# GLA's key and query projections among the convolved tiles, and both halves of an HGRN head's level tree together

## The chip, the cores and the metric

The kernel runs on one core of a Trainium2 chip. The metric is the time of one execution in microseconds of the device, the median of several runs. The profiles are of single executions of the same program, with the records of every engine: TensorE (PE, its weight loads PEld), VectorE (DVE), ScalarE (ACT), GpSimd (POOL) and the engine that issues the DMAs (SP).

## The reference

A two-layer encoder trunk over 1024 tokens of width 1024, float32. Each layer projects the residual stream into the inputs of four token mixers, which run on the same input; each mixer's output is gated, the four are concatenated (2048 wide), projected back and normalized.

```
for i in range(DEPTH):
    h = einsum('bsd,dn->bsn', x, w_in[i])            # all mixers' inputs
    y_a = attention_branch(...)                      # 8 heads of 64, 2 key heads, softmax over 1024
    y_h = hgrn2_branch(...)                          # 4 heads, 128 wide, gated scan in both directions
    y_s = ssd_branch(...)                            # Mamba-2: depthwise convolution, then a scan both ways
    y_g = gla_branch(...)                            # 4 heads, keys of 64, gated scan both ways
    out = einsum('bsn,nd->bsd', concatenate(...), w_out[i])
    x = layer_norm(ALPHA * x + out, ln_g[i], ln_b[i])
```

The gated scan of HGRN and GLA is `S_t = diag(exp(g_t)) S_{t-1} + k_t v_t^T`, `o_t = S_t^T q_t`, forward and backward, summed.

## The kernel before

All time runs along the free dimension: a tile of 128 channels by 512 tokens is one half, and everything is done for half 0 (tokens 0 to 511) and half 1. A projection of 128 channels (`proj` with a PSUM tile of both halves, `projh` with one tile a half) multiplies each 128x128 block of weights with the stream as a high and a low part: `whi` by `xh`, `whi` by `xl`, `wlo` by `xh`, 8 blocks each, 24 matmuls of 512 columns a half. A weight tile comes by DMA (`wraw`), ACT makes `whi`, POOL makes `wlo`. Most results are stored to DRAM (`hdr`) and loaded again by the mixer that needs them.

**The stages of a layer**: attention; HGRN, head after head; SSD; GLA; and the output projection (`oproj`), in pieces by half and branch, which runs beside GLA. Then the LayerNorm and the next layer.

**The level tree** (`tree`, line 649) is how HGRN and GLA do the scan inside chunks of 128 tokens. For one half of a head it makes 32x32 products of keys and queries on TensorE (`lv`), first for single positions (`lv<-q,ks`), then for level sizes 1, 2, 4, 8, 16; for 32 and 64 the products are 64 wide. After each level VectorE multiplies keys (`M`, `C`), queries (`QP`) and decays (`T`) on to the next level and copies a masked part of the products into `near`, while ACT copies a part of `C` into the new `M`. The next level's products read the new `M` and `QP`. `scan_unit` (line 722) does it for half 1 (`second_half`, then its backward states), then for half 0 (`rest`), then the states and the output `ot`. `nh` is the number of heads in the 128 channels: 1 for HGRN, 2 for GLA.

**What sets the order.** The engines' queues are in order, and the program that writes the instructions is a planner. Projections are items of one list, `fill`; the mixers' steps are generators in twelve lanes. A generator yields a list of what its next instructions need: tiles, free PSUM banks ("A:2" is two free banks of the small kind), free buffers ("k2:4"), conditions. The planner keeps a clock for each engine out of fixed costs by size (class `Plan`, line 130) and estimates from it when each tile is ready (`when`, line 547). `run` (line 591) takes a mixer's step when that time has come by TensorE's planned clock, and a step of the current projection otherwise. A yield is no wait on the chip; it only decides what is emitted first. The real waits come from the data.

**The other places that the change touches.** `s_conv` (line 1257) projects one of eight tiles of SSD's input and convolves it: one ACT pass and four VectorE passes over 1024 columns. `s_mix` (line 1377) does the scan of two SSD heads: states `sP` out of `xw` (POOL), the part inside chunks `yd`, the part of the states `yo`; VectorE multiplies `yo` by `off` into `ytmp`, and POOL adds `ytmp` to the sum `u`. `h_stat` (line 1075) normalizes HGRN's output on VectorE and multiplies it by the gate on POOL. `spill` (line 1101) projects a tile with one PSUM tile of both halves, `spill_halves` (line 1112) with one for each half; both store it.

The list of GLA's early projections is line 32:

```
AFILL = ("gk", "gq")
```

Those four tiles stand in `fill` behind GLA's gate tiles and may run as soon as the layer's stream is there (line 1898); the planner used two of them in HGRN of layer 0, and in layer 1 one ahead of HGRN and two in it.

Of the kernel before, what the change touches and what calls it, by code (L numbers as in the profile page):

```python
# [31 lines left out]
AFILL = ("gk", "gq")  # L32
# [285 lines left out]
def hybrid_trunk(ctx, tc, xT_d, wt_d, wo_d, pk_d, w2_d, gain_d, masks_d, imask_d, tri_d, ident_d, rope_d, lnr_d, out_d):  # L318
# [330 lines left out]
    def tree(ins, nh, out):  # L649
        T1, Mk, C, q = ins  # L650
        ins.clear()
        kk = 128 // nh
# [4 lines left out]
        yield [ks, q, f"A:{nh}"]  # L657
# [17 lines left out]
        yield [Mk, QP, f"A:{nh}"]  # L675
# [3 lines left out]
        for lvl, h in enumerate(LEVELS):  # L679
# [39 lines left out]
            yield [M2, QP] + ([f"A:{nh}"] if h < 32 else [])  # L719
        out.update(QP=QP, M=Mk, C=C, T=T, AT=AT)  # L720

    def scan_unit(halves, nh, emit_o):
# [32 lines left out]
        def second_half():  # L755
            yield halves[1][0]
            yield from tree(halves[1][0], nh, un[1])
            yield from states(1, 1, None, Sb)
            first[0] = True

        def rest():
            yield halves[0][0]
            yield from tree(halves[0][0], nh, un[0])
# [63 lines left out]
    def layer(li):  # L827
# [10 lines left out]
        def pc(name, j=0):  # L838
            o = PK[name][0] + j
            return pk[:, o:o + 1]  # L840
# [234 lines left out]
        def h_stat():  # L1075
            for hf in (0, 1):
                r = yield from rstd_of(("o", hf), "hss", 1.0 / (128 * 512), math.log(0.5 * 128.0 ** -0.5))
                for n in range(4):
                    yield ["k2:5"]
                    z = load(("hz", n), hf, "zs")  # L1080
                    o = load(("o", n), hf, "o")
                    yield [z, o, r]
                    ve.scalar_tensor_tensor(out=o, in0=o, scalar=pc("hnorm", n), in1=r, op0=ALU.mult, op1=ALU.mult)
                    tt(gp, o, o, z, ALU.mult)
                    store_y(512 + n * 128, hf, o)
# [291 lines left out]
        def s_mix(n):  # L1377
            def gen():
# [43 lines left out]
                for hf in (0, 1):  # L1422
# [12 lines left out]
                    for d, Ss in ((0, Sf), (1, Sb)):  # L1435
# [7 lines left out]
                        tb = k2("ytmp")  # L1443
                        tt(ve, tb[:, z], yo[:, z], offb[d][:, z], ALU.mult)
                        tt(gp, ta[:, z], ta[:, z], tb[:, z], ALU.add)
# [444 lines left out]
        for g in range(2):  # L1890
            F(f"sB{li}{g}", s_conv(4 + g), after=[f"hp{li}3"], ws=[wsrc("sB", g)])
            F(f"sC{li}{g}", s_conv(6 + g), after=[f"hp{li}3"], ws=[wsrc("sC", g)])
            for n in (2 * g, 2 * g + 1):
                F(f"sx{li}{n}", s_conv(n), after=[f"hp{li}3"], ws=[wsrc("sx", n)])
        for nm in ("gz",):
# [13 lines left out]
        for nm, kind, cnt in (("gk", "raw", 2), ("gq", "raw", 2), ("gv", "tok", 4), ("sz", "silu", 4)):  # L1909
# [101 lines left out]
```

## Time and profile before

| what | value |
|---|---|
| median of 3 runs | 2555.42 us (2553.99 to 2556.37) |
| the profiled execution's own time | 2557.98 us |
| its span, first to last instruction | 2556.2 us |
| TensorE busy | 2420.9 us, 95% |
| VectorE, ScalarE, POOL busy | 1642.6, 1074.9, 971.6 us |
| mean granted TensorE clock | 0.981 |
| HBM read, written | 205.39 MB, 75.96 MB |

A row of a group has the engine, the operation, what it writes and reads, the shape and the count; then the busy time of the group in us, the mean of one in ns, the idle time of the engine just before, and who ended it. A row of the time line has the start and the length in us of one instruction or of a run of equal ones, and in brackets the idle time before it. Matmuls overlap in these records: what one costs is the distance from its start to the next one's. A row of busy time by stretch has, for each engine, busy us and instructions, then the granted clock, the DMA engines' share and GB/s. A matmul in float32 counts as two instructions, so 16 products of a level are `x32`.

### The profile page before, as it was taken

How to read it: one execution, taken by the hardware profiler on the slowest of the kernel's cores; microseconds unless marked ns; L12 is line 12 of the kernel's file. 1: busy time of each engine (PE TensorE's matmuls, PEld its weight loads, DVE VectorE, ACT ScalarE, POOL GpSimd, SP SyncE). 2: the span in 40 equal slices, each digit the busy share in tenths (PEclk: the TensorE clock that was granted, in tenths of full speed). 3: DMA queues.
4: the chain of work that ended last, by engine and by line, in shares of the span. 5: the costliest groups of instructions: out<-in, count | busy, mean ns of one | idle time of the engine just before them, and what ended most of it. 6: DMA issues, size and time to landing. Idle time of an engine off the chain costs nothing. (4 is left out here: it accounts for less than half of the span.)

```text
span 2556.2 us, 46533 instructions
## 1 busy us (share of the span) xinstructions
PE 2420.9 (95%) x18352; PEld 1828.7 (72%) x18352; DVE 1642.6 (64%) x2975; ACT 1074.9 (42%) x2092; POOL 971.6 (38%) x820
## 2 busy tenths in 40 slices
PE   8999999999999996999899999999999999998995
PEld 6767556777778885667777675557777788876774
DVE  2467755453488779774644686554645787887756
ACT  4564555333334334244345545443333243443442
POOL 4432111222225456454464331122223236574444
PEclk9999999999999998999999999999999999999998
DMA  6222111111126547643252311111111156687332
GB/s 222 96 92 66 54 54 46 38 51 51 42 92 213 183 140 277 203 128 97 92 184 80 108 49 59 58 46 38 50 42 51 63 180 203 197 270 235 109 100 91
DMA packets 170174, 284.39 MB, mean 111 GB/s; under 512 B 17780, under 2 KB 43380, under 8 KB 169956
## 3 DMA queue, kind: packets, MB, share of 16 engines
q1 hardware_dynamic: 169956, 281.41, 33.7%
q8 instruction: 145, 2.38, 0.4%
q14 instruction: 73, 0.60, 0.1%
HBM read 205.39 MB, written 75.96 MB: 110 GB/s over the span
## 5 line engine op out<-in xcount | busy, mean ns | idle before, releaser
L312 POOL TENSOR_TENSOR wlo<-wraw,whi 128x512 fp32r<-128x512 f32 x372 | 523.9, 1431 | 716.9 <-ACT whi L312 677.0
L312 PE MATMUL proj<-xh,whi 128*128 128x512 f32 x1056 | 430.4, 408 | 5.1 <-ACT whi L312 5.1
L312 PE MATMUL proj<-xl,whi 128*128 128x512 f32 x1056 | 414.1, 392 | 0.0
L312 PE MATMUL projh<-xh,whi 128*128 128x512 f32 x704 | 289.4, 411 | 16.0 <-ACT whi L312 14.7
L312 PE MATMUL projh<-xl,whi 128*128 128x512 f32 x704 | 281.1, 399 | 1.0 <-DVE xl L312 1.0
L312 PE MATMUL proj<-xh,wlo 128*128 128x512 f32 x1056 | 280.9, 398 | 0.0
L312 ACT CAST whi<-wraw 128x512 fp32r<-128x512 f32 x372 | 213.7, 622 | 114.7 <-DMA wraw<-in_wt 53.6
L312 PEld LDWEIGHTS proj<-xh,whi 128*128 128x128 f32 x1056 | 199.0, 188 | 53.7 <-issue 7.0
L312 PEld LDWEIGHTS proj<-xl,whi 128*128 128x128 f32 x1056 | 199.2, 189 | 38.0 <-issue 1.0
L312 PE MATMUL oproj<-mxh,whi 128*128 128x512 f32 x512 | 216.3, 422 | 9.5 <-ACT whi L312 8.8
L312 PEld LDWEIGHTS proj<-xh,wlo 128*128 128x128 f32 x1056 | 192.4, 188 | 39.4 <-issue 0.5
L312 PE MATMUL oproj<-mxl,whi 128*128 128x512 f32 x512 | 204.1, 399 | 2.8 <-DVE mxl L312 1.6
L312 ACT ACTIVATE Pt<-ST 128x512 f32<-128x512 f32 x256 | 151.3, 599 | 130.6 <-PE ST L312 130.0
L312 PE MATMUL projh<-xh,wlo 128*128 128x512 f32 x704 | 191.4, 395 | 0.0
L312 PEld LDWEIGHTS projh<-xh,whi 128*128 128x128 f32 x704 | 135.7, 193 | 61.9 <-ACT whi L312 16.8
L312 ACT COPY M<-C 128x256 f32<-128x256 f32 x168 | 69.5, 416 | 249.3 <-DVE C L312 240.9
L312 DVE TENSOR_TENSOR QP<-QP,T 128x512 f32<-128x512 f32 x168 | 147.8, 880 | 36.9 <-PE lv L312 35.5
L312 DVE TENSOR_TENSOR psum<-psum,Pt 128x1024 f32<-128x1024 f32 x96 | 121.4, 1265 | 69.0 <-ACT Pt L312 67.8
L312 DVE TENSOR_REDUCE mx<-S 128x1 f32<-128x1024 f32 x128 | 152.7, 1218 | 19.8 <-PE S L312 19.1
L312 PE MATMUL oproj<-mxh,wlo 128*128 128x512 f32 x512 | 151.3, 409 | 6.5 <-POOL wlo L312 6.5
L312 PEld LDWEIGHTS projh<-xl,whi 128*128 128x128 f32 x704 | 136.0, 193 | 27.7 <-DVE xl L312 1.5
L312 PEld LDWEIGHTS projh<-xh,wlo 128*128 128x128 f32 x704 | 129.6, 188 | 30.4 <-issue 4.1
(241 smaller groups left out, 4399.1 us busy)
## 6 DMA issues: line engine op xcount, KB each, us to landing
wraw<-in_wt SPq DMA_DIRECT2D x244, 256.0 KB
wraw<-in_wo SPq DMA_DIRECT2D x128, 256.0 KB
hdr<-zs SPq DMA_DIRECT2D x64, 256.0 KB
zs<-hdr SPq DMA_DIRECT2D x64, 256.0 KB
bc<-dr SPq DMA_DIRECT2D x64, 256.0 KB
yld<-yd SPq DMA_DIRECT2D x56, 256.0 KB
hdr<-sp SPq DMA_DIRECT2D x40, 256.0 KB
yd<-o SPq DMA_DIRECT2D x40, 256.0 KB
```

Of the source, the lines that this page charges most:

```text
L312: return real(*args, **kw)
```

## The change

1. `AFILL` is empty. The four tiles of GLA's keys and queries go, as whole tiles of both halves, into the list of SSD's convolved tiles, one behind each second one: B, C, x, q, x, q, and so on with k in the second group. They may run when the last HGRN head is projected.
2. With one head in the channels (HGRN), `second_half` runs the trees of both halves as two generators in step, half 1 first: the emission of one level for half 1, the same level for half 0, then one common wait for what both need next. `tree` gets `nb`, the number of PSUM banks to ask for. `rest` then only has states and outputs. GLA stays as it was.
3. Each level's step also waits, by the planner's clock, for `C`.
4. Waits by the clock: in `s_mix` for `yo` and `off` ahead of `ytmp`, and for `ytmp` ahead of POOL's addition; in `h_stat` for `o` ahead of POOL's multiplication by the gate.

No matmul and no element is added or dropped.

```diff
-AFILL = ("gk", "gq")
+AFILL = ()
...
-    def tree(ins, nh, out):
+    def tree(ins, nh, out, nb=None):
         T1, Mk, C, q = ins
         ins.clear()
+        nb = nb or nh
...
-        yield [ks, q, f"A:{nh}"]
+        yield [ks, q, f"A:{nb}"]
...
-        yield [Mk, QP, f"A:{nh}"]
+        yield [Mk, QP, f"A:{nb}"]
...
-            yield [M2, QP] + ([f"A:{nh}"] if h < 32 else [])
+            yield [M2, QP, C] + ([f"A:{nb}"] if h < 32 else [])
...
         def second_half():
             yield halves[1][0]
-            yield from tree(halves[1][0], nh, un[1])
+            if nh == 1:
+                yield halves[0][0]
+                two = [tree(halves[hf][0], nh, un[hf], 2) for hf in (1, 0)]
+                while two:
+                    need = []
+                    for g in list(two):
+                        w = next(g, None)
+                        if w is None:
+                            two.remove(g)
+                        else:
+                            need += w
+                    if need:
+                        yield need
+            else:
+                yield from tree(halves[1][0], nh, un[1])
             yield from states(1, 1, None, Sb)
             first[0] = True
 
         def rest():
-            yield halves[0][0]
-            yield from tree(halves[0][0], nh, un[0])
+            if nh > 1:
+                yield halves[0][0]
+                yield from tree(halves[0][0], nh, un[0])
...
                     ve.scalar_tensor_tensor(out=o, in0=o, scalar=pc("hnorm", n), in1=r, op0=ALU.mult, op1=ALU.mult)
+                    yield [o]
                     tt(gp, o, o, z, ALU.mult)
...
                         tb = k2("ytmp")
+                        yield [yo, offb[d]]
                         tt(ve, tb[:, z], yo[:, z], offb[d][:, z], ALU.mult)
+                        yield [tb]
                         tt(gp, ta[:, z], ta[:, z], tb[:, z], ALU.add)
...
             for n in (2 * g, 2 * g + 1):
                 F(f"sx{li}{n}", s_conv(n), after=[f"hp{li}3"], ws=[wsrc("sx", n)])
+                F(f"gq{li}{n}" if n < 2 else f"gk{li}{n - 2}", spill((("gq", n) if n < 2 else ("gk", n - 2)), "raw"), after=[f"hp{li}3"],
+                  ws=[wsrc("gq", n) if n < 2 else wsrc("gk", n - 2)])
...
-        for nm, kind, cnt in (("gk", "raw", 2), ("gq", "raw", 2), ("gv", "tok", 4), ("sz", "silu", 4)):
+        for nm, kind, cnt in (("gv", "tok", 4), ("sz", "silu", 4)):
```

How the planner's order comes out at three places. TensorE in the first HGRN head of layer 0, where `lv` are a level's products and `proj` is the next head's projection; before:

```order
L312 MATMUL lv<-QP,M 32x32 x16
L312 MATMUL proj<-xh,whi 128x512
L312 MATMUL proj<-xl,whi 128x512
L312 MATMUL proj<-xh,whi 128x512
L312 MATMUL proj<-xl,whi 128x512
L312 MATMUL lv<-QP,M 32x32 x16
L312 MATMUL proj<-xh,whi 128x512
L312 MATMUL proj<-xl,whi 128x512
L312 MATMUL proj<-xh,wlo 128x512 x4
L312 MATMUL lv<-QP,M 32x32 x16
L312 MATMUL proj<-xh,wlo 128x512 x4
```

and now, from the head's first burst on:

```order
L312 MATMUL lv<-q,ks 32x32 x32
L312 MATMUL proj<-xh,whi 128x512
L312 MATMUL proj<-xl,whi 128x512
L312 MATMUL proj<-xh,whi 128x512
L312 MATMUL proj<-xl,whi 128x512
L312 MATMUL lv<-QP,M 32x32 x32
L312 MATMUL proj<-xh,whi 128x512
L312 MATMUL proj<-xl,whi 128x512
L312 MATMUL proj<-xh,whi 128x512
L312 MATMUL proj<-xl,whi 128x512
L312 MATMUL proj<-xh,wlo 128x512 x8
```

The 16 products of half 0 stand directly behind those of half 1 (x32 in one row), and half 0's own bursts, which followed further down, are gone.

TensorE at the end of SSD in layer 0, where the last projections (`proj`) meet the first output projection (`oproj`); `yd`, `yo` and `sP` are SSD's; before:

```order
L312 MATMUL yd<-Wm,xt 64x128 x8
L312 MATMUL yo<-u,S 128x128 x7
L312 MATMUL proj<-xh,whi 128x512
L312 MATMUL proj<-xl,whi 128x512
L312 MATMUL proj<-xh,whi 128x512
L312 MATMUL proj<-xl,whi 128x512
L312 MATMUL proj<-xh,whi 128x512
L312 MATMUL proj<-xl,whi 128x512
L312 MATMUL proj<-xh,wlo 128x512 x8
L312 MATMUL sP<-xw,Bt 128x128 x3
L312 MATMUL oproj<-mxh,whi 128x512
```

and now:

```order
L312 MATMUL proj<-xh,whi 128x512
L312 MATMUL proj<-xl,whi 128x512
L312 MATMUL proj<-xh,whi 128x512
L312 MATMUL proj<-xl,whi 128x512
L312 MATMUL proj<-xh,wlo 128x512 x8
L312 MATMUL oproj<-mxh,whi 128x512
```

No row of SSD stands any more among the last projection tile's matmuls or behind them.

The DMA queue (SP) at that same place; `M`, `q`, `T` and `V` are GLA's loads, `yld` loads branch outputs for the output projection, `wraw<-in_wo` its weights, `off` rows for SSD; before:

```order
L312 DMA off<-dro 64x512 x4
L312 DMA M<-hdr 128x512
L312 DMA q<-hdr 128x512
L312 DMA T_9129<-hdr 128x512 x2
L312 DMA yld<-yd 128x512 x4
L312 DMA V<-hdr 128x512 x2
L312 DMA M<-hdr 128x512
L312 DMA q<-hdr 128x512
L312 DMA T_9163<-hdr 128x512 x2
L312 DMA wraw<-in_wo 128x512 x4
```

and now:

```order
L312 DMA yld<-yd 128x512 x4
L312 DMA zs<-hdr 128x512
L312 DMA hdr<-u 128x512
L312 DMA yld<-yd 128x512 x4
L312 DMA M<-hdr 128x512
L312 DMA q<-hdr 128x512
L312 DMA T_9232<-hdr 128x512 x2
L312 DMA wraw<-in_wo 128x512 x4
L312 DMA yld<-yd 128x512 x4
```

SSD's `off` loads stand further up now, and four `yld`, `M`, `q` and two `T` are between the earlier `yld` and the first output weights.

## The prediction

> **What bounds the kernel now.** I read the page first (engines, slices), then busy time by stretch, then the groups and the time line in the stretches that the change touches.
>
> ```profile
> PE 2420.9 (95%) x18352; PEld 1828.7 (72%) x18352; DVE 1642.6 (64%) x2975; ACT 1074.9 (42%) x2092; POOL 971.6 (38%) x820
> PE   8999999999999996999899999999999999998995
> ```
>
> TensorE is busy 95% of the span: time is saved either by fewer nanoseconds of TensorE per matmul or out of the 135 us (2556.2 - 2420.9) in which it idles. Where these lie:
>
> ```profile
> core 0: us, PE busy (x) PEld busy (x) DVE busy (x) ACT busy (x) POOL busy (x), PEclk, DMA share, GB/s
> 440.00:768.00 328.00, 319.82 (x3175) 250.43 (x3174) 179.32 (x370) 109.50 (x228) 89.35 (x89) 1.00 0.17 55
> 768.00:965.00 197.00, 196.81 (x1110) 165.59 (x1109) 152.37 (x330) 78.43 (x156) 98.97 (x80) 1.00 0.59 184
> 965.00:985.00 20.00, 4.23 (x14) 3.13 (x13) 19.75 (x38) 8.92 (x20) 9.99 (x8) 0.64 0.99 344
> 985.00:1220.00 235.00, 218.69 (x2769) 165.54 (x2769) 163.93 (x271) 88.28 (x164) 127.28 (x109) 0.97 0.47 156
> 2240.00:2450.00 210.00, 193.18 (x2621) 144.88 (x2620) 166.04 (x307) 79.65 (x153) 113.77 (x102) 0.98 0.58 188
> ```
>
> In layer 0 the first row is HGRN, the second SSD, the fourth GLA; the third is the seam between SSD and GLA. HGRN and SSD leave TensorE 8.2 and 0.2 us of idle time, so what is cheaper there on TensorE shortens the run one for one. The seam loses 15.8 us of 20, GLA 16.3 us (layer 1: 16.8). The last row is GLA of layer 1, whose seam has no such hole.
>
> **Part 1: both halves of an HGRN head level by level.** Nothing is computed less. One half's burst of 32x32 matmuls (`lv`) in a projection's stream, a burst of the 64-wide levels, and a GLA burst, which is twice as long:
>
> ```profile
> 501.38 0.39 PE L312 MATMUL proj<-xh,whi 128*128 128x512 f32 x1
> 501.60 0.39 PE L312 MATMUL proj<-xl,whi 128*128 128x512 f32 x1
> 501.92 0.47 PE L312 MATMUL lv<-QP,M 128*32 128x32 f32 x32
> 502.32 0.50 PE L312 MATMUL proj<-xh,whi 128*128 128x512 f32 x1
> 502.66 0.40 PE L312 MATMUL proj<-xl,whi 128*128 128x512 f32 x1
> 515.26 0.39 PE L312 MATMUL proj<-xl,whi 128*128 128x512 f32 x1
> 515.58 0.69 PE L312 MATMUL lv<-QP,M 128*64 128x64 f32 x16
> 516.20 0.50 PE L312 MATMUL proj<-xh,whi 128*128 128x512 f32 x1
> 516.53 0.39 PE L312 MATMUL proj<-xl,whi 128*128 128x512 f32 x1
> 990.21 0.76 PE L312 MATMUL lv<-q,ks 64*32 64x32 f32 x64 [0.76 <-POOL ks L312]
> 990.89 0.50 PE L312 MATMUL oproj<-mxh,whi 128*128 128x512 f32 x1
> ```
>
> Matmuls overlap, so I count from start to start. A projection matmul takes 0.22 to 0.23 (501.38 to 501.60). From there the steps are 0.32, 0.40, 0.34: entering the burst costs 0.09, leaving it 0.11, the burst itself 0.40. Two bursts made one save one entry and one exit, 0.20 us, for certain. GLA's 64 instructions take 0.68, not 2 x 0.40, so up to 0.12 more is possible; GLA's rows use half the array's height, so I go half way: 0.25. The 64-wide burst has 0.09, 0.62, 0.10; its 16 instructions run at 39 ns each, with no sign that a second set would be cheaper: 0.20 (at most 0.20 + 0.62, were the second set free).
>
> A head has 1 + 5 + 2 bursts a half, so 8 fall away; of 8 heads, 64: 48 x 0.25 + 16 x 0.20 = **-15 us**. Bounds: 64 x 0.19 = -12 and 48 x 0.32 + 16 x 0.82 = -28.
>
> What hides a level's arithmetic is the projection work between bursts. The first layer's HGRN rows:
>
> ```profile
> L312 DVE TENSOR_TENSOR QP<-QP,T 128x512 f32<-128x512 f32 x56 | 45.3, 810 | 10.3 <-PE lv L312 9.7
> L312 DVE TENSOR_TENSOR M<-M,T 128x256 f32<-128x256 f32 x56 | 29.8, 532 | 0.2
> L312 DVE TENSOR_TENSOR C<-M,T 128x256 f32<-128x256 f32 x56 | 27.6, 492 | 5.7 <-ACT M L312 5.7
> L312 DVE TENSOR_TENSOR T<-T 128x512 f32<-128x512 f32 (+6 forms) x56 | 21.8, 389 | 0.0
> L312 DVE COPY_PREDICATED near<-masks,lv 128x128 f32<-128x128 uint32 x40 | 11.8, 296 | 0.0
> L312 PE MATMUL lv<-QP,M 128*32 128x32 f32 (+1 forms) x1536 | 30.0, 206 | 4.0 <-DVE QP L312 3.7
> L312 PE MATMUL lv<-q,ks 128*32 128x32 f32 x256 | 3.7, 198 | 0.9 <-DVE q L312 0.8
> L312 PE MATMUL lv<-QP,M 128*32 128x32 f32 (+1 forms) x1536 | 30.0, 206 | 3.7 <-DVE QP L312 3.2
> L312 PE MATMUL lv<-q,ks 128*32 128x32 f32 x256 | 3.7, 198 | 1.2 <-DVE q L312 1.0
> ```
>
> (The last two are layer 1's.) VectorE spends 136.3 us on 56 half-levels, 2.43 us each. In the order before, a first tree has 42 projection matmuls and six bursts between its first and last level: 42 x 0.23 + 6 x 0.60 = 13.3 us of TensorE against 6 x 2.43 = 14.6 us of VectorE (overstated, as successive records overlap). That excess of 10% went with 9.8 us of stalls before `lv` in both layers. The changed order has 88 matmuls and six joint bursts: 88 x 0.23 + 6 x 0.90 = 25.6 us against 12 x 2.43 = 29.2 us, an excess of 14%. The other half's steps cover the handovers between engines, but twice as much must fit into a step: I add **+3 us** of stalls. Bounds: -10 (none left) and +30 (rival A).
>
> **Part 2: GLA's key and query projections.** The same 192 matmuls a layer, whole tiles in place of halves, now one behind each second convolved tile. HGRN doesn't miss its share: the order has the next head's projection in that place. SSD gets two tiles more of cover in layer 0 (2 x 48 x 0.23 = 22 us), three in layer 1. Its mixing, in a stretch where VectorE is busy 152 of 197 us, then ends inside the projections: the changed order has the last SSD matmul ahead of the last projection tile, and nothing of SSD behind it. The seam before:
>
> ```profile
> 963.50 2.00 PE L312 MATMUL proj<-xh,wlo 128*128 128x512 f32 x8
> 966.74 0.35 SPq L312 DMA_DIRECT2D M<-hdr  x1
> 968.26 2.66 POOL L312 TENSOR_TENSOR u<-u,ytmp 128x384 f32<-128x384 f32 x2 [2.26 <-DVE ytmp L312]
> 970.88 1.49 POOL L312 TENSOR_TENSOR xw<-xt,colB 128x512 f32<-128x512 f32 x1
> 972.43 1.65 PE L312 MATMUL sP<-xw,Bt 128*128 128x128 f32 x6 [6.94 <-POOL xw L312]
> 976.82 2.35 SPq L312 DMA_DIRECT2D wraw<-in_wo  x4
> 982.90 0.79 PE L312 MATMUL oproj<-mxh,whi 128*128 128x512 f32 x1 [8.83 <-ACT whi L312]
> 983.92 0.63 PE L312 MATMUL oproj<-mxh,whi 128*128 128x512 f32 x1
> 984.35 0.63 PE L312 MATMUL oproj<-mxl,whi 128*128 128x512 f32 x1
> ```
>
> The hole has two causes. 6.94 us: SSD's states wait for `xw`, behind two additions that POOL could not start until `ytmp` was there. That goes. 8.83 us: the output projection waits for weights whose loads were issued at 976.82, 10 us after `M`, behind fourteen GLA and `yld` loads (that one included). In the changed order eight stand there, four of them `yld`, and they still wait for the last projections to free their buffers, so most of this wait stays: I take 1 us off. **-8 us.** Bounds: 0 (the wait finds another owner) and -16 (the seam closes).
>
> By those rows a matmul takes 0.43 us after the hole, for some 14 matmuls, 2.8 us in all. [...]
>
> What is late next is GLA of layer 0. In the order before, its last TensorE work, the `gss` of its last output, stood 107 matmuls ahead of the third piece of the output projection, which needs that output; now 11 stand between.
>
> ```profile
> 1186.80 1.12 PE L312 MATMUL gss<-sq,ones 128*128 128x512 f32 x2
> 1196.16 0.47 PE L312 MATMUL oproj<-mxh,whi 128*128 128x512 f32 x1 [0.49 <-DVE acc L312]
> ```
>
> Before, no long wait followed. 11 x 0.23 = 2.5 us must now cover a normalization and a split (by nearest rows two ACT steps and a cast of 0.6, two VectorE of 0.9 and 1.1, a POOL one of 1.4: some 5.2 plus handovers). **+4 us**; bounds 0 and +20 (all the old cover, 107 x 0.23, missed). In layer 1 GLA ends 76 matmuls earlier than it did, 17 us more cover for the 16.8 us of idle time there, mostly waits inside its own chain: **-2 us**, bounds 0 and -8.
>
> **Part 3: three waits by the clock.** They put no wait on an engine; the planner only emits `ytmp`, its addition and HGRN's gating when their inputs should be there, and POOL gets other work first. On TensorE I count this at nothing beyond the 6.94 us above: what POOL waits for is covered by TensorE's stream elsewhere (0.2 us of idle time in 197). If that cover fails, another 7 us like 972.43 is the price, inside part 2's bound of 0.
>
> **Sum.** -15 + 3 - 8 + 4 - 2 = -18 us on the profiled execution's 2557.98 us (span 2556.2), so 2540.0. The median shown, 2555.42, is 2.6 lower: **2537 us.**
>
> **Rivals.** A, slower: the joint chain becomes HGRN's bound. Each joint step then lasts what VectorE needs, 29.2 us a head against 25.6: 3.6 x 8 = +29 in place of +3, and 2564. It decides from a joint step of 4.3 us on (25.6 / 6). For it: the measured 4.87 of VectorE work a step. Against it: the same excess per half cost 9.8 us before, and the idle time before `QP` (10.3 us) is largely the wait for `lv` that a second half fills. [...]
>
> B, no change: the holes move. The seam keeps its length (0), GLA's end costs +12, the bursts give their least, -12, stalls +3: +3 us, 2558. For it: all of the seam's DMA bursts still come at the end of the projections. Against it: HGRN's 12 us have little to be lost to before the seam.
>
> C, more: bursts -20, no added stalls, seam -14, GLA -2: -36, 2519. For it: two of the three causes were measured at their lower ends.
>
> That the change doesn't do what it says is out for the bursts: the order has 120 in place of 187 `lv` bursts.
>
> **Chances.** Forecast 0.55 (2525 to 2550), C 0.20, B 0.13, A 0.12. A difference of 0.2% (5 us) is about the least that can be told from none. Faster 0.75, same 0.13, slower 0.12. The range, 2512 to 2558, leaves out A's upper part and C's lower end.
>
> **What would show it.** `lv` rows with x64 and x32 in HGRN and about 0.2 us less per pair; `lv` idle time of 10 to 15 us over the two stretches (over 35: A); the first output projection of layer 0 waiting under 9 us with no `sP` wait ahead; a wait of some 4 us at layer 0's third piece. I am wrong if HGRN's two stretches aren't some 6 us shorter each at equal work, or if the seam still loses 15 us.

## The result and the profile after

The changed kernel takes 2536.55 us (median of 4 runs, 2534.32 to 2538.76) against 2555.71 us before (4 runs): a ratio of 0.9924, 95% interval 0.9911 to 0.9936. The forecast was 2537, in a range from 2512 to 2558, with faster at 0.75. The total is right; its split, as will be seen, is not, so that the hit is in good part luck.

The profiled execution took 2534.32 us. Its page has:

```profile
PE 2389.7 (94%) x18352; PEld 1827.7 (72%) x18352; DVE 1639.2 (65%) x2975; ACT 1080.4 (43%) x2098; POOL 981.3 (39%) x820
```

Its span is 2532.5 us and its mean granted clock 0.986 (0.981 before). TensorE is busy 31.2 us less (2420.9 before) and idle 142.8 us (135.3 before): the span fell by 23.7 us because the same matmuls cost less, and in spite of more waiting. By stretch, in the changed kernel (three of HGRN's four heads in layer 0; the last projection tile up to the first output projection; from there to the piece that takes GLA's half 0, which the prediction calls the third and which is the fifth of six in the kernel's list; the last projection tile up to the next layer's first projection; three of HGRN's heads in layer 1):

```profile
core 0: us, PE busy (x) PEld busy (x) DVE busy (x) ACT busy (x) POOL busy (x), PEclk, DMA share, GB/s
473.40:672.90 199.50, 190.60 (x2217) 156.85 (x2216) 113.69 (x258) 68.60 (x152) 57.13 (x58) 1.00 0.13 41
955.10:975.80 20.70, 11.06 (x50) 8.84 (x48) 8.86 (x12) 8.11 (x16) 5.14 (x4) 0.90 0.77 272
975.80:1192.40 216.60, 205.25 (x2709) 156.22 (x2710) 152.09 (x260) 86.63 (x161) 118.39 (x99) 0.99 0.50 166
955.10:1258.30 303.20, 273.59 (x3045) 212.29 (x3043) 208.51 (x386) 117.16 (x212) 156.14 (x126) 0.97 0.47 158
1725.10:1925.10 200.00, 190.61 (x2218) 156.73 (x2216) 119.22 (x270) 68.68 (x152) 59.81 (x58) 1.00 0.13 41
```

The same five stretches before:

```profile
472.10:696.30 224.20, 220.09 (x2314) 174.00 (x2312) 115.40 (x258) 73.92 (x160) 61.26 (x62) 1.00 0.14 46
950.70:982.90 32.20, 16.44 (x93) 13.40 (x91) 27.53 (x67) 11.86 (x25) 10.80 (x8) 0.81 0.92 297
982.90:1212.60 229.70, 213.39 (x2739) 161.30 (x2740) 163.13 (x268) 88.75 (x165) 125.14 (x106) 0.96 0.49 161
950.70:1274.10 323.40, 284.24 (x3103) 218.99 (x3101) 233.64 (x443) 120.85 (x222) 163.84 (x135) 0.94 0.49 162
1763.90:1988.00 224.10, 220.09 (x2314) 173.99 (x2312) 122.14 (x270) 73.96 (x160) 61.58 (x62) 1.00 0.14 46
```

**HGRN.** Before, each of its stretches held 96 projection matmuls more, 21.8 us at 0.227 each. At equal work TensorE's busy time falls from 198.3 to 190.6, by 7.7 us a layer, and its idle time rises from 4.1 to 8.9 us (layer 0) and from 4.0 to 9.4 (layer 1). These three heads gain 2.9 and 2.3 us. Ahead of `lv`, over all four heads of both layers, TensorE idles 22.5 us in place of 9.8; in layer 0:

```profile
L312 PE MATMUL lv<-QP,M 128*32 128x32 f32 (+1 forms) x1536 | 27.0, 205 | 10.7 <-DVE QP L312 10.7
```

Where it waits, TensorE in the first head:

```profile
483.83 0.47 PE L312 MATMUL lv<-QP,M 128*32 128x32 f32 x32
485.10 0.46 PE L312 MATMUL lv<-QP,M 128*32 128x32 f32 x32 [0.81 <-DVE QP L312]
```

The 16 products of half 1 run at once; those of half 0, in the same burst, wait for `QP`. VectorE at that time:

```profile
480.92 1.14 DVE L312 TENSOR_TENSOR QP<-QP,T 128x512 f32<-128x512 f32 x1
481.90 0.62 DVE L312 TENSOR_TENSOR C<-M,T 128x256 f32<-128x256 f32 x1
482.46 0.67 DVE L312 TENSOR_TENSOR T<-T 128x512 f32<-128x512 f32 x1
483.05 0.28 DVE L312 COPY_PREDICATED near<-masks,lv 128x128 f32<-128x128 uint32 x1
483.25 0.63 DVE L312 TENSOR_TENSOR M<-M,T 128x256 f32<-128x256 f32 x1
483.81 1.14 DVE L312 TENSOR_TENSOR QP<-QP,T 128x512 f32<-128x512 f32 x1
```

The two `QP` at 480.92 and 483.81 belong to half 1 and half 0 of one level. Between them VectorE still does half 1's `C`, `T` and `near`, which only the next level needs, and half 0's `M`. The burst of 483.83 waits in its middle, until 485.10.

**The seam of layer 0.** TensorE's time line:

```profile
975.78 0.80 PE L312 MATMUL oproj<-mxh,whi 128*128 128x512 f32 x1 [9.64 <-ACT whi L312]
976.38 0.63 PE L312 MATMUL oproj<-mxl,whi 128*128 128x512 f32 x1
976.80 0.63 PE L312 MATMUL oproj<-mxh,whi 128*128 128x512 f32 x1
```

There is no `sP` with its wait any more, and one wait of 9.64 us is left: 6.1 us less idle time than the 15.8 before.

**GLA of layer 0** gains more than its seam. Here is `yo`, TensorE's last work in SSD, from the last projections on, in the kernel before:

```profile
L312 PE MATMUL yo<-u,S x28: 275/275/377, 960.4 to 1006.2; 128*128 128x128 f32 x28
```

and in the changed one:

```profile
L312 PE MATMUL yo<-u,S x14: 271/275/275, 948.9 to 951.3; 128*128 128x128 f32 x14
```

Before, the last `yo` came 23 us after the first output projection (982.90), inside GLA's first trees; now 24 us ahead of it. The 108 us of GLA that start 21 us behind the first output projection, before:

```profile
1004.00:1112.00 108.00, 96.04 (x1493) 72.42 (x1494) 84.56 (x151) 37.92 (x71) 53.44 (x47) 0.94 0.56 186
```

and after:

```profile
997.00:1105.00 108.00, 104.24 (x1328) 79.48 (x1329) 70.59 (x125) 40.43 (x74) 58.46 (x51) 1.00 0.57 192
```

VectorE is busy 14 us less, TensorE idle 3.8 us in place of 12.0, and the granted clock 1.00 in place of 0.94. (The two stretches are equally long but don't hold the same work: 1493 matmul records before, 1328 now.) Over the whole stretch from the last projection tile to the next layer 20.2 us are gained: 10.7 of TensorE's busy time, of which 5.4 is the work of SSD that left it at the seam (16.44 - 11.06), and 9.6 of idle time.

### The profile page after: what moved, and what is told of

Read it like the earlier page. It is cut to its first block, busy times and chain, and to the rows that moved or that the text cites. A ratio compares the mean times of both kernels' runs of the same rounds, so it can differ in the third digit from the quotient of the medians.

```text
span 2532.5 us, 46526 instructions
## 1 busy us (share of the span) xinstructions
PE 2389.7 (94%) x18352; PEld 1827.7 (72%) x18352; DVE 1639.2 (65%) x2975; ACT 1080.4 (43%) x2098; POOL 981.3 (39%) x820
## 4 chain that ended last, share of the span: by engine, by line
PE 42%; DVE 8%; ACT 2%; issue 2%; DMA 2%; POOL 0%; SPq 0%; DVEq 0%; ACTq 0%; POOLq 0%
PE proj L312 13%; PE oproj L312 8%; PE projh L312 7%; PE O L312 2%; PE ST L312 2%; PE ot L312 2%; DVE QP L312 1%; PE lv L312 1%; PE S L312 1%; PE P L312 1%; DVE mxl L312 1%; DVE C L312 1%; DVE xt L312 1%; DVE acc L312 1%; DVE M L312 1%
## 5 line engine op out<-in xcount | busy, mean ns | idle before, releaser
L312 PE MATMUL proj<-xh,whi 128*128 128x512 f32 x1184 | 482.1, 407 | 11.3 <-ACT whi L312 11.2
L312 PE MATMUL proj<-xl,whi 128*128 128x512 f32 x1184 | 464.6, 392 | 0.0
L312 PE MATMUL proj<-xh,wlo 128*128 128x512 f32 x1184 | 309.6, 396 | 0.0
L312 PEld LDWEIGHTS proj<-xh,wlo 128*128 128x128 f32 x1184 | 217.6, 188 | 45.4 <-issue 1.8
L312 PE MATMUL projh<-xh,whi 128*128 128x512 f32 x576 | 234.4, 407 | 16.5 <-ACT whi L312 15.9
L312 PE MATMUL projh<-xl,whi 128*128 128x512 f32 x576 | 228.7, 397 | 1.0 <-DVE xl L312 1.0
L312 PE MATMUL projh<-xh,wlo 128*128 128x512 f32 x576 | 155.4, 394 | 0.0
L312 PEld LDWEIGHTS projh<-xh,whi 128*128 128x128 f32 x576 | 110.4, 192 | 56.5 <-ACT whi L312 18.5
L312 PEld LDWEIGHTS lv<-QP,M 128*32 128x32 f32 (+3 forms) x6144 | 81.5, 114 | 77.0 <-issue 57.5
L312 PE MATMUL lv<-QP,M 128*32 128x32 f32 (+3 forms) x6144 | 97.2, 206 | 36.0 <-DVE QP L312 24.4
```

The lines of the kernel that those rows point to most:

```text
L312: return real(*args, **kw)
```

## The experiments

Two readings stood against each other. In the first (theory S in the expectations; T has the same with the sizes that the two traces show) each part is worth its own terms, and the parts add. In the second (E) a part's worth hangs on where SSD's last mixing falls: ahead of GLA, or among its chains. A third (P) was that the holes move by chance with every change of the order. After the first answers two more questions were open: which part of the joint trees costs the stalls, and whether the hole at the seam costs anything. None of the kernels leaves out any of the computation.

| kernel | median, us | ratio to before, interval |
|---|---|---|
| joint trees only | 2582.13 | 1.0101 (1.0088 to 1.0115) |
| move of `gk`, `gq` only | 2560.43 | 1.0023 (1.0012 to 1.0033) |
| waits by the clock only | 2562.54 | 1.0030 (1.0018 to 1.0042) |
| all but the joint trees | 2552.30 | 0.9988 (0.9979 to 0.9997) |
| all but the move | 2545.67 | 0.9966 (0.9955 to 0.9978) |
| all but the waits | 2556.43 | 1.0009 (0.9998 to 1.0019) |
| `gk`, `gq` behind all convolved tiles | 2539.93 | 0.9944 (0.9932 to 0.9957) |
| bursts apart again | 2529.07 | 0.9899 (0.9886 to 0.9912) |
| `QP` of both halves first | 2518.89 | 0.9858 (0.9841 to 0.9876) |
| the same, no wait for `C` | 2557.43 | 1.0013 (1.0003 to 1.0023) |
| seam's weights early | 2538.98 | 0.9936 (0.9924 to 0.9949) |
| `QP` first, weights early | 2520.87 | 0.9867 (0.9855 to 0.9880) |

### One part alone

Joint trees with the wait for `C`, on the kernel before:

```diff
-            yield [M2, QP] + ([f"A:{nh}"] if h < 32 else [])
+            yield [M2, QP, C] + ([f"A:{nb}"] if h < 32 else [])
...
+                two = [tree(halves[hf][0], nh, un[hf], 2) for hf in (1, 0)]
```

> Before, with the joint HGRN trees alone (parts 2 and 3 of the list: trees in step, the wait for C by the clock). Theory S, the prediction's split: 64 bursts fewer save 15 us, stalls cost 3, so 2555.7 - 12 = 2544, and HGRN's two stretches are 6 us shorter each. Theory T, the split that the two traces show: entries and exits save 16 us, but TensorE waits inside the joint bursts for half 0's QP, so only some 5 us are left: 2551, with HGRN 2.5 us shorter per layer. Theory P, the holes between the stages move by chance with every change of the order: anything from 2540 to 2560, with seams and GLA that differ from both traces.

The move alone:

```diff
-AFILL = ("gk", "gq")
+AFILL = ()
...
+                F(f"gq{li}{n}" if n < 2 else f"gk{li}{n - 2}", spill(...), after=[f"hp{li}3"], ...)
```

> Before, with GLA's key and query projections moved between the convolved tiles, and nothing else. Theory S: the seam between SSD and GLA of layer 0 loses 8 us less, GLA's end 4 more, layer 1 2 less: 2550, with no 6.9 us wait of sP. Theory T: 6 us at the seam and some of the 20 us that the changed kernel gains between layer 0's GLA and layer 1's attention: 2540 to 2548. Theory P: 2545 to 2562.

The waits alone:

```diff
+                    yield [o]
                     tt(gp, o, o, z, ALU.mult)
...
+                        yield [yo, offb[d]]
                         tt(ve, tb[:, z], yo[:, z], offb[d][:, z], ALU.mult)
+                        yield [tb]
```

> Before, with the waits by the clock in s_mix and h_stat alone. Theory S: nothing beyond noise, 2553 to 2557, or 7 us less if the 6.9 us wait of sP at layer 0's seam goes by this alone. Theory T: the same. Theory P: up to 8 us either way.

Measured: each part alone makes the kernel **slower**, by 26.5, 4.8 and 6.9 us. Their sum, +38, has the other sign than the whole, -19: the parts don't add at all. Of the expectations, only theory P, the widest, holds for the move and for the waits; none had the joint trees' 2582. In HGRN itself the joint trees do gain there, some 4 us a layer at equal work (three heads take 218.8 and 219.2 us in place of 224.2 and 224.1, and 0.9 us of each difference are eight transposes that fall outside the stretch). What the joint trees alone lose, they lose in GLA of layer 1. SSD's last matmul, and the stretch from that layer's first output projection to GLA's last matmul (`gss`), first by the tile's own view (durations, first and last start), then by stretch:

```profile
L312 PE MATMUL yo<-u,S x224: 270/275/582, 807.6 to 2316.9; 128*128 128x128 f32 x112
```

```profile
2229.53:2505.50 275.97, 241.69 (x2848) 182.56 (x2846) 205.04 (x363) 99.39 (x194) 134.59 (x119) 0.91 0.50 163
```

The projections end 14 us earlier than before (2229.5 against 2243.5), yet SSD's mixing ends 32 us later (2316.9 against 2284.8), 87 us deep in GLA. VectorE is busy 205 us in that stretch, TensorE idles 34.3 us and runs at a granted 0.91. The same two rows of the changed kernel:

```profile
L312 PE MATMUL yo<-u,S x224: 270/275/377, 781.6 to 2213.1; 128*128 128x128 f32 x112
```

```profile
2228.20:2440.40 212.20, 193.47 (x2646) 145.08 (x2645) 149.90 (x263) 84.72 (x160) 108.38 (x94) 0.98 0.55 187
```

SSD is done 15 us ahead of GLA, which takes 212 us in place of 276, with VectorE busy for 150.

### One part left out

The joint trees taken back out of the changed kernel (the lines of the first diff above, reversed):

```diff
-                two = [tree(halves[hf][0], nh, un[hf], 2) for hf in (1, 0)]
+            yield from tree(halves[1][0], nh, un[1])
```

> The changed kernel without the joint trees: the move and the waits in s_mix and h_stat, HGRN's halves one after the other as before. Theory S: 2536.6 + 12 = 2549. Theory T: 2536.6 + 5 = 2541 to 2543. Theory P: off both by more than 6 us.

The move taken back:

```diff
-AFILL = ()
+AFILL = ("gk", "gq")
...
-        for nm, kind, cnt in (("gv", "tok", 4), ("sz", "silu", 4)):
+        for nm, kind, cnt in (("gk", "raw", 2), ("gq", "raw", 2), ("gv", "tok", 4), ("sz", "silu", 4)):
```

> The changed kernel without the move of GLA's key and query projections (joint trees and all waits by the clock stay). Theory E, that came out of the first runs: the end is the later of two, TensorE's remaining stream, or layer 1's last GLA output plus 75 us; without the move SSD of layer 1 ends 40 to 90 us behind the last projection and GLA sets the end. So it is slower than the changed kernel by 20 to 45 us, 2557 to 2580, SSD's last matmul lies over 40 us behind the last projection, and from GLA's last output to the end it is 73 to 77 us. Rival P, chance of the planner's order: no slower than 2550.

The waits taken back (the wait for `C` stays):

```diff
-                    yield [o]
...
-                        yield [yo, offb[d]]
-                        yield [tb]
```

> The changed kernel without the waits by the clock in s_mix and h_stat (move and joint trees stay). Theory E: the move alone keeps SSD inside the projections, so TensorE's stream sets the end and the waits are worth little: 2535 to 2545, SSD's last matmul ahead of the last projection's end, 85 us or more from GLA's last output to the end. Rival: the waits are what brought SSD forward; then 2550 or more, with 75 us at the end. In the runs so far the move alone is at 2560.4, and move with these waits at 2552.3.

Measured: 2552.3, 2545.7 and 2556.4 us. Beside the two others, the joint trees are worth -15.7 us, the move -9.1, the waits -19.9. Read from the traces as above for all eight combinations (columns: SSD's last `yo` behind (+) or ahead of (-) the first output projection of layer 1; from there to the last `gss`, and TensorE's idle time in it; from the last `gss` to the span's end):

| parts | median, us | last `yo` | to `gss` (idle) | then to the end |
|---|---|---|---|---|
| none | 2555.6 | +41 | 238 (17) | 75 |
| joint | 2582.1 | +87 | 276 (34) | 73 |
| waits | 2562.5 | +87 | 270 (31) | 76 |
| joint, waits | 2545.7 | +57 | 224 (16) | 86 |
| move | 2560.4 | -17 | 220 (22) | 88 |
| move, joint | 2556.4 | -28 | 232 (21) | 73 |
| move, waits | 2552.3 | -11 | 210 (16) | 91 |
| all | 2536.6 | -15 | 212 (19) | 92 |

With the move SSD is over ahead of layer 1's output projection in all four, and without it in none; for layer 1 that was not among the prediction's terms. (It isn't a rule: with the output weights early, further down, SSD ends 13 us behind, in spite of the move.) The second reading holds so far. As a rule for the time it fails: its numbers for the last two kernels missed. Without the move, the kernel was to be no faster than before; it is 9 us faster, with `yo` 57 us inside GLA. Without the waits it was to be near the changed kernel; it is 19.9 us slower. Layer 1's GLA isn't where: its last `gss` comes 20 us later, but what follows is as much shorter, and from the first output projection to the end it is 305.9 us against 304.3. The time goes in layer 0. Two stretches have it: from the fourth head's first burst to the last projection tile, in which SSD lies, and from the first output projection to the piece that takes GLA's half 0:

```profile
673.30:961.30 288.00, 280.20 (x1910) 232.97 (x1910) 222.96 (x464) 108.16 (x209) 129.25 (x107) 0.98 0.50 156
982.20:1210.30 228.10, 209.38 (x2709) 159.29 (x2710) 150.91 (x261) 86.62 (x160) 112.17 (x98) 0.96 0.47 157
```

In the changed kernel the first of these is

```profile
674.90:955.10 280.20, 275.24 (x1909) 229.13 (x1909) 223.20 (x464) 108.26 (x209) 127.20 (x108) 1.00 0.50 161
```

and the second is 216.60 us, with the same number of matmuls: 7.8 and 11.5 us.

The kernel without the joint trees has the changed kernel's work in HGRN, so that it prices them there directly:

```profile
470.76:672.36 201.60, 198.40 (x2218) 155.91 (x2216) 117.14 (x258) 69.38 (x152) 55.35 (x58) 1.00 0.13 41
```

Joint, the same three heads take 199.5 us: 7.8 us of busy time less, 5.7 of idle time more, 2.1 gained (1.7 in layer 1). That is a little less than the 2.9 and 2.3 above, as TensorE's idle time without the joint trees is 3.2 us here and was 4.1 there. Most of their 15.7 us lies elsewhere, in the stretch from layer 0's last projection tile to the next layer's first projection. That is 323.4 us before, 315.9 without the joint trees, 316.2 without the move, 315.6 without the waits, and 303.2 only with all three. Why the third part, whichever comes last, takes another 12 to 13 us off it was not traced to one cause and stays open; that it is the chance of one order is not excluded.

### Inside the joint trees

Both halves' `M` and `QP` of a level first, then `C`, `T` and `near` of both, in `tree` behind the multiplication that makes `QP`:

```diff
             tt(ve, qa, qa, AV(T, nblk + 1, [[2, ng2], [-nblk - 1, 2], [0, h]]), ALU.mult)
+            if nh == 1:
+                yield []
             rb = [[4 * h, ng4], [h, 2], [1, h]]
```

> The changed kernel with another order of a joint level on VectorE: M and QP of both halves first, then C, T and near of both. The next burst needs M and QP alone. Theory T: the waits inside the joint bursts (TensorE for half 0's QP, some 20 us over both layers by the two traces) fall by more than half and the kernel gains 5 to 12 us: 2525 to 2532; HGRN's two stretches are 4 us shorter each. Rival: VectorE's throughput over the whole level is the bound, not the place of QP in it, and nothing changes: 2533 to 2540.

Both trees in step, but each with its own wait, so that projection matmuls come between the two halves' bursts (181 bursts in place of 120):

```diff
                         if w is None:
                             two.remove(g)
                         else:
-                            need += w
-                    if need:
-                        yield need
+                            yield w
```

> The changed kernel with both halves' trees in step, but each half's step waits by the clock on its own, so the two halves' bursts stand apart in TensorE's stream (181 bursts in place of 120). Theory S: what pays is the entry and exit of a burst, 0.20 us each pair; 61 more bursts cost 12 us, less what the waits inside the joint bursts cost: the net is some 0 to 8 us slower, 2537 to 2545, and HGRN's stretches have the entries back but fewer waits. Rival: running the halves side by side is the gain, not the burst; no slower than 2537.

HGRN's stretches with `QP` first:

```profile
471.20:665.00 193.80, 190.14 (x2218) 156.76 (x2216) 112.92 (x258) 68.43 (x152) 55.12 (x58) 1.00 0.13 42
1719.80:1914.00 194.20, 190.44 (x2218) 156.72 (x2216) 119.37 (x270) 68.36 (x152) 58.58 (x58) 1.00 0.13 42
```

and with the bursts apart:

```profile
471.50:668.40 196.90, 196.90 (x2218) 155.89 (x2216) 117.61 (x258) 67.90 (x152) 55.32 (x56) 1.00 0.12 39
1724.40:1921.50 197.10, 197.10 (x2216) 155.82 (x2215) 126.04 (x270) 68.13 (x152) 57.89 (x58) 1.00 0.12 39
```

The work is equal in these and in the changed kernel. Apart, TensorE never idles and is busy 6.3 and 6.5 us longer: 12.8 us. These stretches hold 95 bursts in place of 48 (the 61 more are those of the whole program), so one burst more costs 0.27 us. That is its price, on its own. And HGRN is still 2.6 and 2.9 us shorter than in the changed kernel, and the kernel 7.5 us faster, where the expectation had it up to 8 slower: **the joint burst cost more in stalls than it saved in bursts.** With `QP` first both are had: busy 190, idle 3.7 and 3.8, 5.7 and 5.8 us a layer less. The order on VectorE, in the first head:

```profile
478.70 1.16 DVE L312 TENSOR_TENSOR QP<-QP,T 128x512 f32<-128x512 f32 x1
480.24 1.17 DVE L312 TENSOR_TENSOR QP<-QP,T 128x512 f32<-128x512 f32 x1
481.24 0.64 DVE L312 TENSOR_TENSOR C<-M,T 128x256 f32<-128x256 f32 x1
```

(between the two `QP` stands half 0's `M` alone) and the burst that reads both, in one piece and without a wait:

```profile
481.28 0.39 PE L312 MATMUL proj<-xl,whi 128*128 128x512 f32 x1
481.60 0.77 PE L312 MATMUL lv<-QP,M 128*32 128x32 f32 x64
482.29 0.50 PE L312 MATMUL proj<-xh,whi 128*128 128x512 f32 x1
482.63 0.39 PE L312 MATMUL proj<-xl,whi 128*128 128x512 f32 x1
```

From start to start the steps are 0.32, 0.69 and 0.34 us: 0.09 for going in and 0.11 for going out, as in a burst of one half, but 0.69 for the products, where two bursts of one half took 0.40 each. A joint burst without a wait so saves 0.31 us.

So the stalls come from `C`, `T` and `near` of half 1 ahead of half 0's `QP`, as the time lines suggested. This kernel, at 2518.89 us, is the fastest of all: 0.9858 of before, 17.7 us under the changed one, more than the 5 to 12 expected. Three of HGRN's heads in each layer explain 11.5 of that; over all heads TensorE's idle time ahead of `lv` is 9.0 us, no more than the 9.8 before. The rest was not traced.

The same without the planner's wait for `C`:

```diff
-            yield [M2, QP, C] + ([f"A:{nb}"] if h < 32 else [])
+            yield [M2, QP] + ([f"A:{nb}"] if h < 32 else [])
```

> M and QP of both halves first (the run qp_first, 2518.9), and the planner no longer waits for C ahead of the next joint burst. The wait for C makes the planner put more projection work between the bursts. Theory: with QP early the chip doesn't need that; 0 to 4 us faster than qp_first if C's clock was what spaced the bursts, 2514 to 2519. Rival: less work between them brings waits for QP back: 2520 to 2530.

Measured 2557.43 us, 38.5 more and far outside both expectations, for an edit that puts no wait on any engine. HGRN and SSD of layer 0 in it, and from its time line the longest wait in that SSD:

```profile
471.80:672.60 200.80, 191.12 (x2218) 157.30 (x2216) 113.37 (x258) 68.66 (x152) 56.71 (x58) 1.00 0.12 41
672.60:967.80 295.20, 281.07 (x1920) 233.51 (x1918) 223.94 (x466) 108.97 (x212) 130.37 (x109) 0.98 0.48 153
```

```profile
776.66 0.79 PE L312 MATMUL proj<-xh,whi 128*128 128x512 f32 x1 [7.54 <-ACT whi L312]
```

SSD with `QP` first and the wait for `C` kept:

```profile
665.00:944.70 279.70, 276.51 (x1918) 230.40 (x1917) 223.56 (x466) 110.53 (x213) 128.32 (x108) 1.00 0.50 161
```

HGRN has its stalls back (9.7 us) and SSD idles 14.1 us in place of 3.2, more than half of it one projection that waits for its weights (`whi`, which ACT makes). Taking out the wait for `C`, which GLA's trees have too, costs more than this kernel had gained over the one before (36 us); on the changed kernel itself it was not taken out. That a few instructions emitted in another order are followed by a hole 100 us later is why single edits can't be priced one by one here.

### Place and seam

Keys and queries behind all convolved tiles, in place of between them:

```diff
-                F(f"gq{li}{n}" if n < 2 else f"gk{li}{n - 2}", spill(...), after=[f"hp{li}3"], ...)
...
-        for nm, kind, cnt in (("gv", "tok", 4), ("sz", "silu", 4)):
+        for nm, kind, cnt in (("gk", "raw", 2), ("gq", "raw", 2), ("gv", "tok", 4), ("sz", "silu", 4)):
```

> The changed kernel with the four key and query projections behind all eight convolved tiles, ahead of GLA's values, in place of between them; the same whole tiles, as late as before. Theory E: what counts is how much projection work is left when SSD's mixing can run; it is the same, so 2533 to 2545. Rival B, between counts: a convolved tile needs four VectorE passes of 1.28 us, and eight in a row hold VectorE back; then TensorE waits for PSUM banks or SSD starts later, and it is slower by 5 us or more.

Measured 2539.93 us, as expected, 3.4 more than the changed kernel and 5.7 less than without the move. So most of the move's 9.1 us comes with the tiles behind HGRN, wherever they stand among SSD's; their place is worth some 3.4, and the two intervals of the ratios still overlap.

The first output weights loaded and split ahead of their turn, and the same with `QP` first:

```diff
-PRE = ('hp0', 'hp1', 'o1')
+PRE = ('hp0', 'hp1', 'o0', 'o1')
```

> The changed kernel, with the first weights of layer 0's output projection loaded ahead of its turn as those of layer 1 are (their loads stand seven rows further up in the DMA queue, ahead of the yld and GLA loads). The prediction counted the 8.8 us wait for these weights as staying. Theory: the wait (9.6 us in the changed kernel) goes but for 1 to 3 us, and the slow clock behind it too: 2526 to 2532. Rival: the branch loads (yld) are as late as the weights, TensorE then waits for the split mxh or mxl, and 0 to 3 us are gained: 2533 to 2540.

> qp_first and pre_o0 together. If both act in their own place: qp_first's 2518.9 less what pre_o0 gives on the changed kernel, 2508 to 2519. Rival, the order moves elsewhere: above 2520.

The last projection tile of layer 0, and from the first output projection to the piece that takes GLA's half 0, with early weights on the changed kernel:

```profile
956.00:966.80 10.80, 10.80 (x49) 8.96 (x48) 4.88 (x6) 4.93 (x9) 6.91 (x5) 1.00 0.62 217
966.80:1194.20 227.40, 206.25 (x2710) 155.51 (x2708) 155.75 (x268) 91.91 (x169) 111.25 (x99) 0.98 0.51 175
```

The hole is closed: the first output projection follows directly. And the two stretches together last 238.2 us, against 237.3 in the changed kernel with its hole (20.70 + 216.60). The 9.6 us come back as idle time between the later matmuls, 21.2 us (227.40 - 206.25) in place of 11.4. Half of them are the same wait again, at the next output weights:

```profile
974.39 0.50 PE L312 MATMUL oproj<-mxh,whi 128*128 128x512 f32 x1 [1.96 <-ACT whi L312]
989.54 0.50 PE L312 MATMUL oproj<-mxh,whi 128*128 128x512 f32 x1 [2.94 <-ACT whi L312]
```

New besides are, above all, two waits of 2.5 us in GLA, ahead of `kst`, for `C`. Output projections and GLA share that stretch; that GLA's own chain sets its length fits this but isn't shown. By this stretch the hole costs nothing, and both kernels are level with their partners: 2539.0 beside 2536.6, 2520.9 beside 2518.9. (The first is the rival's number, but not for the rival's reason; the second lies just in its rival's range.) But the level times are themselves a sum. From layer 0's last projection tile to the next layer's first projection, the two kernels with early weights are 3.0 and 6.3 us shorter than their partners (with 16 and 15 matmul records fewer in it), and from there to layer 1's first HGRN burst both are 11.2 us longer (480.8 against 469.6, 481.3 against 470.1). Whether the hole as such costs time is therefore not settled.

## Why the prediction came out as it did

**The bursts, -15 us: right in kind, too small.** HGRN's busy time at equal work fell by 7.7 us a layer, 15.3 in all, but in three of four heads. That is 0.32 us for each of 48 bursts, and some -20 us for all 64 (15.3 x 64 / 48, an estimate). The prediction took 0.25 and 0.20. Entry and exit are as it read them; the closer running of 64 instructions, which it took at half, came in full, and the 64-wide bursts, in which it saw no sign of any, have it too: around the joint one at 506.93 in the changed kernel the steps from start to start are 0.32, 1.08 and 0.33 us (506.61 to 508.34), 1.27 more than two projection matmuls at 0.23; two separate ones took 2 x 0.81.

**The stalls, +3 us: the step that failed.** The idle time ahead of `lv` rose from 9.8 to 22.5 us, by 12.7 (10.2 in the stretches above, 4.8 and 5.4). The excess of VectorE's work over TensorE's was used as if the order inside a level were indifferent, and "the other half's steps cover the handovers" was taken from that. But a joint burst needs the second half's `QP`, and the order put three operations of the first half ahead of it. VectorE's load is the same with `QP` first (112.92 us against 113.69) and POOL's nearly so (55.12 against 57.13), and there the idle time stayed at 3.7 in the stretch. The mechanism that rival A named, the joint chain, was there at under half of its +29, and it was a matter of order, not of load. The test set in advance, HGRN some 6 us shorter a layer, failed with it: 2.9 and 2.3 in three heads, under 4 with the fourth. So did its second sign: 22.5 us idle ahead of `lv`, where 10 to 15 were named, though far from the 35 of rival A.

**The seam, -8 us: right as a size, open as a gain.** `sP` lost its wait, the first output projection kept its own, and 6.1 us of idle time went. Whether a hole there is on the path that sets the end isn't settled: with the remaining 9.6 us closed, the stretch up to GLA's half 0 kept its length, but half of them came back at the next weights. That most of the 6.1 were gained as such can't be said either.

**GLA of layer 0, +4 us: wrong, it is 0.** The piece that takes GLA's half 0 now:

```profile
1192.37 0.39 PE L312 MATMUL oproj<-mxh,whi 128*128 128x512 f32 x1
```

No wait stands ahead of it, 3.1 us behind the last `gss` (1189.24). That last `gss` belongs to half 1, and this piece takes half 0's output, whose last `gss` starts at 1172.29, 20 us ahead: the distance counted in the order was between two things of which one doesn't need the other. (Before, this piece starts at 1212.60; the row at 1196.16 is in the piece ahead of it.)

**GLA of layer 1, -2 us: not there.** From layer 1's first output projection to the end, TensorE's idle time goes from 42.8 to 44.6 us. That this stretch is 8.4 us shorter (304.3 in place of 312.7) is busy time, 10.2 us less, with SSD's last products gone from it.

**What the sum lacked.** TensorE's busy time fell by 31.2 us, of which some 20 are the bursts'. By the mean granted clock, 0.981 before and 0.986 now, and with matmuls 0.43 us apart in place of 0.23 while the clock is at 0.50 (last section), some 97 us ran at half clock before and 71 now; half of the difference, 13 us, is TensorE time. This is an estimate, and an upper one, as TensorE may idle in such time. It lies mostly in the stretch of layer 0's seam and GLA, where the clock went from 0.94 to 0.97 over 300 us. The prediction had the clock at 2.8 us, at the seam alone. The order showed SSD gone from behind layer 0's last projections; that this leaves VectorE to GLA's first trees was not used, only the 6.94 us of `sP`. It is a part of the gain there and not the whole: the move alone takes SSD out of GLA in layer 0 too (the last `yo` 8 us ahead of the first output projection), and shortens the stretch by 6.4 us (317.0) of the 20.2. Together: bursts some -20, clock up to -13, other busy time some +2 (in all -31.2); stalls +12.7, seam's idle time -6.1, other idle time +0.9 (in all +7.5): -23.7 us.

**The waits by the clock, 0: wrong.** They are worth -19.9 us beside the other two parts, in layer 0's SSD and GLA, and +6.9 alone. The reason given, that POOL's waits are covered by TensorE's stream, speaks of one kernel's order; it can't price a change to the rule by which the order is made.

So the forecast met the medians (2537 against 2536.55; they lie 19.2 us apart) by errors that partly cancel, which is luck: the stalls cost some 10 us more than counted; the bursts saved some 5 more, the 4 us at GLA's end were not there, and up to 13 us of the clock were not counted. Its own execution's time it missed by 6 us (2540.0 against 2534.32). And its sum was built on parts that add, which the eight combinations refute. Of the rivals, B (the holes move) comes near what four of the other seven combinations do, which gain nothing: with `gk` and `gq` moved and the trees joint, but without the waits, the time is 2556.4, B's price within 2 us. C was put at 2519; the kernel with `QP` first takes 2518.89. Two of C's terms are in it, bursts of some -20 and no added stalls; its -14 at the seam is not (9.9 us of idle time there, in place of 15.8).

**The clock at the seam.** The granted clock fell with the hole and not without one: behind the 9.64 us it is at 0.50 (975.78 to 979.20) and the first matmuls are 0.43 us apart (976.38 to 976.80), and with early weights the seam's clock is 1.00 (956.00 to 966.80). In GLA it also fell with shorter waits (last section).

## What to carry to other kernels

When two chains share a burst, emit first what the burst of both needs, and only then what each chain needs for its next step (here 2518.89 us against 2536.55); the joint bursts, of which one half came late, cost more here than two bursts each (2536.55 us against 2529.07 with the bursts apart). Ask of a hole whether the stretch around it is as long as the hole makes it or as long as another chain makes it: fill it once, and see whether the idle time comes back further on, and whether the same wait only moves to the next load. Before a stretch's saving is set against a sum, count how many of the heads it holds. Where a planner makes the order, test parts of a change in all combinations, since what one part alone does may have the other sign than what it does beside the rest.

## What was not expected of the hardware

In HGRN a burst of 32x32 products in a stream of 512-column matmuls cost 0.20 us for going in and out, from start to start (0.09 and 0.11, at 501.92 before and at 481.60 with `QP` first), and its products ran closer in a larger burst: 64 instructions in 0.69 us (481.60), 32 in 0.40 (501.92). 47 bursts more at equal work cost 12.8 us, 0.27 each, with TensorE idle for none of it.

The granted clock was also lost where no wait was longer than 2.81 us. A wait of TensorE in GLA of layer 0 before, and the 3.41 us behind it:

```profile
1021.59 1.06 PE L312 MATMUL lv<-QP,M 64*32 64x32 f32 x64 [2.81 <-DVE near L312]
```

```profile
1021.72:1025.13 3.41, 3.41 (x70) 2.83 (x69) 3.41 (x6) 0.44 (x1) 1.09 (x1) 0.50 0.17 32
```

Behind this one wait of 2.81 us the clock is at 0.50 and the matmuls are 0.43 us apart (1024.03 to 1024.46). In the row from 1004 to 1112 above, with its 0.94, no wait is longer; the other drops go with waits of 2.79 and 2.00 us (0.50 from 1072.91 to 1079.74 and from 1096.81 to 1100.22), some 13 us at half clock in all. The changed kernel, idle for 3.8 us there in place of 12.0, keeps 1.00, and it keeps it behind a wait of 2.98 us that ends at 997.07, too. So the clock fell with waits of 2.81, 2.79 and 2.00 us and held behind one of 2.98; what decides it was not measured.
